# Retention scores and state products as 64-row matmuls of two heads into two PSUM banks

## The chip, the cores and the metric

The kernel runs on one core of a Trainium2 chip. The metric is device time in microseconds (us) for one execution. The engines are named as the profile names them: PE is TensorE (matmuls; PEld is its weight load), DVE is VectorE, ACT is ScalarE, POOL is GpSimd, and SP is the queue that issues all DMAs of this kernel.

## The reference

One layer of a streaming encoder over 2048 prompt tokens and 64 sample tokens, model width 1024. Three groups of heads (HGRN2, retention, memory cross-attention) take their columns from one projection of the normalised input; each is multiplied by a gate, and the concatenation goes through an output projection and a final norm. The part at issue is retention: 4 heads, keys of 64, values of 128, in chunks with a carried state.

```
scores = einsum('bcihd,bcjhd->bchij', qc, kc) * intra      # gamma^|n-m| inside a chunk
o  = einsum('bchij,bcjhv->bcihv', scores, vc)
dr = einsum('bcjhd,hj,bcjhv->bchdv', kc, k_decay, vc)
r_{c+1} = chunk_decay * r_c + dr_c                         # the state of each head, 64 x 128
o  = o + einsum('bcihd,hi,bchdv->bcihv', qc, q_decay, r_c)
o_rt = head_group_norm(o, g) * silu(gate)                  # mean and variance over the 128 of a head
```

All results are fp32. The kernel uses chunks of 128 tokens with a mask in the decay table that reproduces the reference's chunks of 64.

## The kernel before

The tokens are worked in two groups of 1024 and 1088 (the second ends with the 64 sample tokens), and within a group projection by projection: retention's gates, then its values, then its queries and keys, then HGRN2, then attention; the output projection comes last. Projections are long runs of matmuls in which a number is split into a high and a low part, three products for one (`gemm_col`, L249, and `gemm_tok`, L294). They make up most of TensorE's work. Everything else is hung between them.

The order on PE and SP is written out by hand. A planner holds a clock, `now`, that is advanced by `pe(us)` behind each matmul with the cost that the author gives it. Side work is a generator that is put up as a task with a due time; each `yield d` ends one section and makes the next due `d` later. `poll()` is called between the steps of a projection (in `gemm_tok` after every three passes of 512 columns but the last three) and runs what is due, earliest first; a section of a task waits until the task before it of the same class is past the same section. The order on DVE, ACT and POOL is chosen by the scheduler of the language, which prefers the sections of tasks.

`retention` (L586) computes the projection of one chunk of 128 tokens, applies the rotary embedding (L602 to L608), makes the decayed keys `kd` (L610), and puts up `retention_tail` (L615), due 6.0 us later. The tail has four sections:

- Section 0: four transposes (L620) put q and k of four heads into a bank `tr` as pairs: rows 0 to 63 hold an even head, rows 64 to 127 the odd one. ACT copies q into `q2` as a block-diagonal (L624, L625): even head in columns 0 to 127 of the upper rows, odd head in columns 128 to 255 of the lower rows, and zeros elsewhere. ACT copies k (L628), DVE makes q times its decay (L630).
- Section 1: for each pair `p` one 128-row matmul of 256 columns gives the scores of two heads at once (L637; four small ones for the sample, L635). All four heads fill the one bank `scb`. DVE multiplies by the decay table into `sd` (L641). Four matmuls on 64 columns of the array each (L647) give the state's increment `db`, two heads in the upper and two in the lower partitions.
- Section 2: for each pair one 128-row matmul with the block-diagonal state `R` (L653), then the two heads' products of `sd` with the values accumulate onto it (L657). All four heads fill the bank `ob`. DVE updates the state from `db` (L666, four operations; L662 in the first chunk, which has no state and no L653), reduces `ob` (L673), scales (L674) and subtracts the mean (L677); ACT squares (L682), POOL takes the power (L237), DVE multiplies (L685).
- Section 3: four transposes (L693), the product with the gate (L695), and a store.

PSUM has eight banks of 512 fp32 columns. `acc()` hands out three, `trp()` two (tag `tr`), `obank()` two (tag `ob`, used for `db` and `ob`, and by HGRN2 and attention), and `scb` is one bank of its own that HGRN2 uses as well. A new tile from a pool waits until a bank of it has been read for the last time.

Of the kernel before, what the change touches and what calls it, by code (L numbers as in the profile page):

```python
# [11 lines left out]
ALU = mybir.AluOpType  # L12
AX = mybir.AxisListType
PSUM = bass.MemoryType.PSUM

P = 128
# [37 lines left out]
D_RT0 = 6.0  # L54
# [9 lines left out]
def layer_kernel(ctx: ExitStack, tc: tile.TileContext, io: dict):  # L64
    nc = tc.nc
    V, S, G, T = nc.vector, nc.scalar, nc.gpsimd, nc.tensor
# [25 lines left out]
    def pe(us):  # L92
        now[0] += us

    def task(cls, gen, delay):
        prev = last.get(cls)
        t = {"t": now[0] + delay, "gen": gen, "prev": prev, "stage": 0}
        last[cls] = t
        pend.append(t)
# [107 lines left out]
    for i in range(2):  # L207
        a = const.tile([P, 512], F32, name=f"abuf{i}")
# [4 lines left out]
    scb = p_sc.tile([P, 512], F32, name="scb")  # L213
# [6 lines left out]
    def slot(dt=F32):  # L220
        return wk.tile([P, 512], dt, tag="s", name="s")
# [7 lines left out]
    def trp():  # L229
        return p_tr.tile([P, 512], F32, tag="tr", name="tr")  # L230

    def obank():
        return p_o.tile([P, 512], F32, tag="ob", name="ob")
# [176 lines left out]
    def subchunks(tok0, nt):  # L410
        out = []
        o = 0
        while o < nt:
            L = 128 if tok0 + o < SEQ else DEC
            out.append((o, L))
            o += L
        return out
# [8 lines left out]
    def bc(ap, shape):  # L426
        return ap.to_broadcast(shape)
# [158 lines left out]
    def retention(ws, ht, tok0, nt, vt, R, dtab, last_tile):  # L586
        for c, (o, L) in enumerate(subchunks(tok0, nt)):
            t = tok0 + o
            ti = t // 128
            ct_ = sm.tile([P, 96], F32, tag="cs", name="cs", bufs=2)  # L590
            dma(ct_[0:L], io["rope"][ti, 0:L])
            cosb = ct_[0:L, 0:32].rearrange("p (a b) -> p a b", a=1)
            nsin = ct_[0:L, 32:64].rearrange("p (a b) -> p a b", a=1)
            sinb = ct_[0:L, 64:96].rearrange("p (a b) -> p a b", a=1)
            ps = gemm_tok(ws, ht, o, L, last_tile and o + L == nt)
            if L == DEC:
                pf = slot()
                fold(pf[0:L], ps)
                ps = pf
            r = slot()  # L600
            tmp = slot()
            V.tensor_tensor(out=r[0:L].rearrange("p (a b) -> p a b", b=32), in0=ps[0:L].rearrange("p (a b) -> p a b", b=32),  # L602
                            in1=bc(cosb, [L, 16, 32]), op=ALU.mult)
            pv = ps[0:L].rearrange("p (a t b) -> p a t b", t=2, b=32)
            tv = tmp[0:L].rearrange("p (a t b) -> p a t b", t=2, b=32)
            V.tensor_tensor(out=tv[:, :, 0, :], in0=pv[:, :, 1, :], in1=bc(nsin, [L, 8, 32]), op=ALU.mult)
            V.tensor_tensor(out=tv[:, :, 1, :], in0=pv[:, :, 0, :], in1=bc(sinb, [L, 8, 32]), op=ALU.mult)
            V.tensor_tensor(out=r[0:L], in0=r[0:L], in1=tmp[0:L], op=ALU.add)  # L608
            kd = slot()
            V.tensor_tensor(out=kd[0:L, 0:256].rearrange("p (h d) -> p h d", h=4), in0=r[0:L, 256:512].rearrange("p (h d) -> p h d", h=4),  # L610
                            in1=bc(kdec[L][0:L].rearrange("p (h o) -> p h o", o=1), [L, 4, 64]), op=ALU.mult)
            task("rt", retention_tail(t, L, vt[c], r, kd, R[0 if L == 128 else 1], dtab), D_RT0)
            poll()

    def retention_tail(t, L, v, r, kd, R, dtab):  # L615
        first = t == 0
        sample = L == DEC
        tr = trp()
        for j in range(4):
            T.transpose(tr[:, j * 128:j * 128 + L], r[0:L, j * 128:(j + 1) * 128], ident[0:L, 0:L])  # L620
            pe(0.107)
        trv = tr.rearrange("p (j l) -> p j l", j=4)
        q2 = q2b[(t // 128) % 2]
        S.copy(q2[0:64, :, 0:L], trv[0:64, 0:2, 0:L])  # L624
        S.copy(q2[64:128, :, 128:128 + L], trv[64:128, 0:2, 0:L])  # L625
        kq = slot()
        kqv = kq.rearrange("p (a b) -> p a b", a=4)
        S.copy(kqv[:, 0:2, 0:L], trv[:, 2:4, 0:L])  # L628
        if not first:
            V.tensor_tensor(out=kqv[:, 2:4, 0:L], in0=trv[:, 0:2, 0:L], in1=qdec[:, :, 0:L], op=ALU.mult)  # L630
        yield D_RT1
        for p in range(2):
            if sample:
                for hh in range(2):
                    T.matmul(scb[0:L, p * 256 + hh * 128:p * 256 + hh * 128 + L], kqv[:, p, 0:L], q2[:, p, hh * 128:hh * 128 + L], start=True, stop=True)  # L635
            else:
                T.matmul(scb[:, p * 256:(p + 1) * 256], kqv[:, p, :], q2[:, p, :], start=True, stop=True)  # L637
            pe(0.426)
        sd = slot()
        sdv = sd.rearrange("p (a b) -> p a b", a=4)  # L640
        V.tensor_tensor(out=sdv[0:L, :, 0:L], in0=scb.rearrange("p (a b) -> p a b", a=4)[0:L, :, 0:L],  # L641
                        in1=dtab.rearrange("p (a b) -> p a b", a=4)[0:L, :, 0:L], op=ALU.mult)
        db = obank()
        dv = db[:, 0:256].rearrange("p (a b) -> p a b", a=2)
        for h in range(4):
            p, hh = h // 2, h % 2
            T.matmul(dv[64 * hh:64 * hh + 64, p, :], kd[0:L, h * 64:(h + 1) * 64], v[0:L, h * 128:(h + 1) * 128], start=True, stop=True)  # L647
            pe(0.213)
        yield D_RT2
        ob = obank()  # L650
        for p in range(2):
            if not first:
                T.matmul(ob[0:L, p * 256:(p + 1) * 256], kqv[:, 2 + p, 0:L], R[:, p, :], start=True, stop=False)  # L653
                pe(0.426)
            for hh in range(2):
                h = 2 * p + hh
                T.matmul(ob[0:L, h * 128:(h + 1) * 128], sdv[0:L, h, 0:L], v[0:L, h * 128:(h + 1) * 128], start=first, stop=first or hh == 1)  # L657
                pe(0.213)
        for hh in range(2):
            sl = slice(64 * hh, 64 * hh + 64)  # L660
            if first:
                V.tensor_copy(R[sl, :, 128 * hh:128 * hh + 128], dv[sl])  # L662
            else:
                for p in range(2):
                    blk = R[sl, p, 128 * hh:128 * hh + 128]
                    V.scalar_tensor_tensor(out=blk, in0=blk, scalar=gcol[L][sl, p:p + 1], in1=dv[sl, p, :], op0=ALU.mult, op1=ALU.add)  # L666
        if sample or t + 128 == SEQ:
            dst = io["o_srt_s"] if sample else io["o_srt_p"]
            for h in range(4):
                p, hh = h // 2, h % 2  # L670
                store(dst[0, 0, h], R[64 * hh:64 * hh + 64, p, 128 * hh:128 * hh + 128], 2.0)
        mu = small(4, "mu")
        V.tensor_reduce(out=mu[0:L], in_=ob[0:L].rearrange("p (a b) -> p a b", a=4), axis=AX.X, op=ALU.add)  # L673
        V.tensor_scalar(out=mu[0:L], in0=mu[0:L], scalar1=1.0 / 128, scalar2=None, op0=ALU.mult)  # L674
        cc = slot()
        ccv = cc[0:L].rearrange("p (a b) -> p a b", a=4)
        V.tensor_tensor(out=ccv, in0=ob[0:L].rearrange("p (a b) -> p a b", a=4),  # L677
                        in1=bc(mu[0:L].rearrange("p (a o) -> p a o", o=1), [L, 4, 128]), op=ALU.subtract)
        ss = small(4, "ss4")
        junk = slot()  # L680
        for h in range(4):
            S.activation(junk[0:L, h * 128:(h + 1) * 128], cc[0:L, h * 128:(h + 1) * 128], AF.Square, accum_out=ss[0:L, h:h + 1])  # L682
        rs = small(4, "rs4")
        rsqrt_small(rs[0:L], ss[0:L], 4, 1.0 / 128, EPS)
        V.tensor_tensor(out=ccv, in0=ccv, in1=bc(rs[0:L].rearrange("p (a o) -> p a o", o=1), [L, 4, 128]), op=ALU.mult)  # L685
        gr = slot()
        grv = gr.rearrange("p (a b) -> p a b", a=4)[:, :, 0:L]
        blk = mixT[1024:1536, t:t + L].rearrange("(a p) l -> p a l", p=P)
        dma(grv, blk)
        yield D_RT3  # L690
        tro = trp()
        for h in range(4):
            T.transpose(tro[:, h * 128:h * 128 + L], cc[0:L, h * 128:(h + 1) * 128], ident[0:L, 0:L])  # L693
            pe(0.107)
        V.tensor_tensor(out=grv, in0=grv, in1=tro.rearrange("p (a b) -> p a b", a=4)[:, :, 0:L], op=ALU.mult)  # L695
        store(blk, grv)
# [153 lines left out]
    start = ExitStack()  # L850
# [341 lines left out]
    for i_, o in enumerate(order):  # L1192
        L = 128 if o < SEQ else DEC
# [113 lines left out]
```

## Time and profile before

| | us |
|---|---|
| median of 3 runs | 1943.49 |
| lowest and highest run | 1939.63, 1945.09 |
| the profiled execution | 1944.17 |
| its span, first to last instruction | 1942.4 |
| PE busy | 1908.9 |
| DVE busy | 1043.3 |
| ACT busy | 585.9 |

The granted TensorE clock was 0.995 over the span. In a row of a timeline stand the start in us, the duration, engine, line, operation, the tiles out<-in, the form of the array that is used (rows*columns), the operands' shape and a count; neighbours of one line are merged. A duration of a PE record holds the latency of the pipeline and overlaps with the next, so what a matmul costs is read from start to start. An fp32 matmul stands as two records. Rows of groups show busy time, mean ns of one, and the engine's idle time ahead of them with what ended it. Rows of one source line show durations in ns as lowest/median/highest, then the first and last start.

### The profile page before, as it was taken

The page shows a single profiled execution, that of the slowest core. Times are in us where ns is not written, and L with a number is a line of the kernel's source. Part 1 is how long each engine was busy: PE and PEld are TensorE (multiplying, and loading weights), DVE is VectorE, ACT ScalarE, POOL GpSimd, SP SyncE. Part 2 cuts the span into 40 slices and gives each one's busy share as a digit, 9 for nine tenths or more (in the row PEclk, how much of TensorE's full clock was granted, in tenths as well). Part 3 has the DMA queues.
Part 4 walks back from the last instruction along what each step waited for, and adds up shares of the span by engine and source line. Part 5 has one row for each costly group of instructions (what it writes and reads, how often), then busy time and mean ns, then how long its engine had stood idle before and what let it go on. Part 6 is the DMA issues. An engine that isn't in the chain of part 4 may idle for free.

```text
span 1942.4 us, 28116 instructions
## 1 busy us (share of the span) xinstructions
PE 1908.9 (98%) x10938; PEld 1618.5 (83%) x10938; DVE 1043.3 (54%) x2512; ACT 585.9 (30%) x1414; POOL 139.9 (7%) x335
## 2 busy tenths in 40 slices
PE   8999999999999999999999999999999999999998
PEld 7888788888888787988789998899989878888886
DVE  8527457753677557417637774477765642222222
ACT  7413232322333434312323332233333431111111
POOL 0001000000100100000101111021100000000000
PEclk9999999999999999999999999999999999999999
DMA  7512222111111424212211111111122342233322
GB/s 254 179 58 55 75 66 61 44 50 44 44 55 55 153 71 134 92 55 58 87 47 49 49 49 49 44 49 49 60 71 78 118 144 87 87 102 113 89 71 60
DMA packets 116742, 153.21 MB, mean 79 GB/s; under 512 B 13312, under 2 KB 79232, under 8 KB 116608
## 3 DMA queue, kind: packets, MB, share of 16 engines
q1 hardware_dynamic: 116608, 151.41, 25.4%
q8 instruction: 86, 1.41, 0.3%
q14 instruction: 48, 0.39, 0.1%
HBM read 117.69 MB, written 33.69 MB: 78 GB/s over the span
## 4 chain that ended last, share of the span: by engine, by line
PE 87%; DVE 6%; DMA 2%; ACT 2%; issue 1%; POOL 1%; SPq 0%; DVEq 0%; POOLq 0%; ACTq 0%
PE acc L249 39%; PE acc L1180 19%; PE acc L294 15%; PE scb L522 2%; PE ob L531 2%; PE ob L563 1%; PE ob L566 1%; PE acc L785 1%; PE ob L741 1%; PE acc L264 1%; PE tr L516 1%; PE tr L581 1%; PE tr L763 1%; DVE wlo L241 1%; ACT s L682 1%
## 5 line engine op out<-in xcount | busy, mean ns | idle before, releaser
L249 PE MATMUL acc<-hb,whi 128*128 128x320 f32 (+2 forms) x1696 | 409.1, 331 | 0.4 <-DVE hb L371 0.4
L249 PE MATMUL acc<-ha,whi 128*128 128x512 f32 x1120 | 354.7, 398 | 0.0
L249 PEld LDWEIGHTS acc<-hb,whi 128*128 128x128 f32 x1696 | 284.6, 189 | 25.0 <-issue 4.4
L241 DVE TENSOR_TENSOR wlo<-wst,whi 128x1024 fp32r<-128x1024 f32 x115 | 140.0, 1226 | 261.2 <-ACT whi L240 260.2
L249 PE MATMUL acc<-hb,wlo 128*128 128x256 f32 (+2 forms) x848 | 276.9, 327 | 0.0
L249 PEld LDWEIGHTS acc<-ha,whi 128*128 128x128 f32 x1120 | 205.0, 189 | 41.3 <-issue 2.6
L249 PE MATMUL acc<-ha,wlo 128*128 128x512 f32 x560 | 220.0, 393 | 0.0
L240 ACT CAST whi<-wst 128x1024 fp32r<-128x1024 f32 x115 | 119.7, 1051 | 211.4 <-PE acc L249 172.0
L249 PEld LDWEIGHTS acc<-hb,wlo 128*128 128x128 f32 x848 | 160.2, 189 | 11.2
L294 PE MATMUL acc<-whi,ha 128*128 128x512 f32 x512 | 161.0, 396 | 0.0
L294 PE MATMUL acc<-whi,hb 128*128 128x512 f32 x512 | 160.0, 394 | 0.0
L1180 PE MATMUL acc<-whi,s 128*128 128x512 f32 x396 | 125.9, 396 | 1.3 <-ACT s L240 1.0
L249 PEld LDWEIGHTS acc<-ha,wlo 128*128 128x128 f32 x560 | 105.7, 189 | 23.1 <-DVE wlo L241 0.2
L294 PEld LDWEIGHTS acc<-whi,hb 128*128 128x128 f32 x512 | 94.5, 188 | 19.8 <-issue 1.2
L294 PEld LDWEIGHTS acc<-whi,ha 128*128 128x128 f32 x512 | 93.8, 188 | 19.6 <-issue 1.3
L294 PE MATMUL acc<-wlo,ha 128*128 128x512 f32 x256 | 100.1, 391 | 0.0
L294 PE MATMUL acc<-wlo,hb 128*128 128x512 f32 x256 | 99.8, 390 | 0.0
L1180 PE MATMUL acc<-hb,s 128*128 128x512 f32 x400 | 97.7, 400 | 0.0
L1180 PE MATMUL acc<-ha,s 128*128 128x512 f32 x400 | 96.3, 396 | 0.0
L1180 PEld LDWEIGHTS acc<-hb,s 128*128 128x128 f32 x400 | 76.3, 191 | 18.4
L241 DVE TENSOR_TENSOR s<-mst,s 128x512 fp32r<-128x512 f32 (+1 forms) x64 | 40.4, 671 | 94.2 <-ACT s L240 94.2
L1180 PEld LDWEIGHTS acc<-whi,s 128*128 128x128 f32 x396 | 74.3, 188 | 19.6 <-ACT s L240 1.3
(236 smaller groups left out, 2913.3 us busy)
## 6 DMA issues: line engine op xcount, KB each, us to landing
wst<-w_in_t SPq DMA_DIRECT2D x104, 512.0 KB, 4.0
mixT<-s SPq DMA_DIRECT2D x64, 256.0 KB, 4.3
mst<-mixT SPq DMA_DIRECT2D x30, 512.0 KB, 5.9
wst<-w_out_t SPq DMA_DIRECT2D x16, 512.0 KB, 4.0
xq<-x_prompt SPq DMA_DIRECT2D x18, 256.0 KB, 5.0
o_yp<-xq SPq DMA_DIRECT2D x18, 256.0 KB, 2.3
s<-mixT SPq DMA_DIRECT2D x16, 256.0 KB, 3.0
s<-x_prompt SPq DMA_DIRECT2D x16, 256.0 KB, 5.3
```

Of the source, the lines that this page charges most:

```text
L240: S.copy(hi, src)
L241: V.tensor_tensor(out=lo, in0=src, in1=hi.bitcast(F32), op=ALU.subtract)
L249: T.matmul(ps[:, 0:nt], w[a][:, kk, :], ht[b][:, kk, 0:nt], start=(n == 0), stop=(n == 23))
L264: T.matmul(ps[:, 0:nt], w[a][:, kk, :], ht[b][:, kk, 0:nt], start=(kk == 0 and a + b == 0), stop=(kk == KT - 1 and a == 1))
L294: T.matmul(ps[0:L, :], ht[b][:, kk, o:o + L], w[a][:, kk % 2, :], start=(n == 0), stop=(n == 23))
L516: T.transpose(trk[:, c * 128:(c + 1) * 128], kch[:, c * 128:(c + 1) * 128], ident)
L522: T.matmul(scb[32 * e:32 * e + 32, c * 128 + 32 * e:(c + 1) * 128], K[:, c * 128 + 32 * e:c * 128 + 32 * e + 32], Qe[:, c, E_OFF[e]:E_OFF[ ...
L531: T.matmul(db[:, c * 128:(c + 1) * 128], kT[:, c * 128:(c + 1) * 128], vt[c], start=True, stop=True)
L563: T.matmul(ob[:, c * 128:(c + 1) * 128], A[:, c * 128:(c + 1) * 128], vt[c], start=True, stop=first)
L566: T.matmul(ob[:, c * 128:(c + 1) * 128], qst[:, c * 128:(c + 1) * 128], st[c][0], start=False, stop=True)
L581: T.transpose(tro[:, c * 128:(c + 1) * 128], on[:, c * 128:(c + 1) * 128], ident)
L1180: T.matmul(ps, m[a][:, kk % 4], w[b], start=(n == 0), stop=(n == 16 * len(terms) - 1))
```

## The change

The scores and the state products are no longer taken for two heads at once through zeros, but one matmul per head on 64 rows of the array (`sl`, rows 0 to 63 for the even head of a pair, 64 to 127 for the odd one), with 128 columns where there were 256. The even heads' results go into one bank and the odd heads' into another: `scb` and a bank of `obank()` for the scores, a bank of `obank()` and one of `trp()` for the outputs. For the sample the state product stays at 128 rows. `q2` holds the pair as it comes, so one ACT copy replaces two. Three DVE operations (L641, L673, L677) become two each. The planner's cost for a pair goes from 0.426 to 0.3, and the sample's tail is put up 2.0 us later.

```
-            task("rt", retention_tail(...), D_RT0)
+            task("rt", retention_tail(...), D_RT0 if L == 128 else D_RT0 + 2.0)
...
-        S.copy(q2[0:64, :, 0:L], trv[0:64, 0:2, 0:L])
-        S.copy(q2[64:128, :, 128:128 + L], trv[64:128, 0:2, 0:L])
+        S.copy(q2[:, :, 0:L], trv[:, 0:2, 0:L])
...
+        sc2 = (scb, obank())
         for p in range(2):
-            if sample:
-                for hh in range(2):
-                    T.matmul(scb[0:L, p * 256 + hh * 128:p * 256 + hh * 128 + L], kqv[:, p, 0:L], q2[:, p, hh * 128:hh * 128 + L], start=True, stop=True)
-            else:
-                T.matmul(scb[:, p * 256:(p + 1) * 256], kqv[:, p, :], q2[:, p, :], start=True, stop=True)
-            pe(0.426)
+            for hh in range(2):
+                sl = slice(64 * hh, 64 * hh + 64)
+                T.matmul(sc2[hh][0:L, p * 128:p * 128 + L], kqv[sl, p, 0:L], q2[sl, p, 0:L], start=True, stop=True)
+            pe(0.3)
...
-        V.tensor_tensor(out=sdv[0:L, :, 0:L], in0=scb.rearrange("p (a b) -> p a b", a=4)[0:L, :, 0:L],
-                        in1=dtab.rearrange("p (a b) -> p a b", a=4)[0:L, :, 0:L], op=ALU.mult)
+        for hh in range(2):
+            V.tensor_tensor(out=sdv[0:L, hh:4:2, 0:L], in0=sc2[hh].rearrange("p (a b) -> p a b", a=4)[0:L, 0:2, 0:L],
+                            in1=dtab.rearrange("p (a b) -> p a b", a=4)[0:L, hh:4:2, 0:L], op=ALU.mult)
...
-        ob = obank()
+        ob2 = (obank(), trp())
         for p in range(2):
             if not first:
-                T.matmul(ob[0:L, p * 256:(p + 1) * 256], kqv[:, 2 + p, 0:L], R[:, p, :], start=True, stop=False)
-                pe(0.426)
+                for hh in range(2):
+                    sl = slice(0, P) if sample else slice(64 * hh, 64 * hh + 64)
+                    T.matmul(ob2[hh][0:L, p * 128:(p + 1) * 128], kqv[sl, 2 + p, 0:L], R[sl, p, 128 * hh:128 * hh + 128], start=True, stop=False)
+                pe(0.3)
             for hh in range(2):
                 h = 2 * p + hh
-                T.matmul(ob[0:L, h * 128:(h + 1) * 128], sdv[0:L, h, 0:L], v[0:L, h * 128:(h + 1) * 128], start=first, stop=first or hh == 1)
+                T.matmul(ob2[hh][0:L, p * 128:(p + 1) * 128], sdv[0:L, h, 0:L], v[0:L, h * 128:(h + 1) * 128], start=first, stop=True)
...
-        V.tensor_reduce(out=mu[0:L], in_=ob[0:L].rearrange("p (a b) -> p a b", a=4), axis=AX.X, op=ALU.add)
+        for hh in range(2):
+            V.tensor_reduce(out=mu[0:L, hh:4:2], in_=ob2[hh][0:L, 0:256].rearrange("p (a b) -> p a b", a=2), axis=AX.X, op=ALU.add)
...
-        V.tensor_tensor(out=ccv, in0=ob[0:L].rearrange("p (a b) -> p a b", a=4),
-                        in1=bc(mu[0:L].rearrange("p (a o) -> p a o", o=1), [L, 4, 128]), op=ALU.subtract)
+        for hh in range(2):
+            V.tensor_tensor(out=ccv[:, hh:4:2, :], in0=ob2[hh][0:L, 0:256].rearrange("p (a b) -> p a b", a=2),
+                            in1=bc(mu[0:L, hh:4:2].rearrange("p (a o) -> p a o", o=1), [L, 2, 128]), op=ALU.subtract)
```

More of the change, by code (lines that the diff above doesn't have):

```diff
@@ L611, in retention @@
                             in1=bc(kdec[L][0:L].rearrange("p (h o) -> p h o", o=1), [L, 4, 64]), op=ALU.mult)
-            task("rt", retention_tail(t, L, vt[c], r, kd, R[0 if L == 128 else 1], dtab), D_RT0)
+            task("rt", retention_tail(t, L, vt[c], r, kd, R[0 if L == 128 else 1], dtab), D_RT0 if L == 128 else D_RT0 + 2.0)
             poll()
```

## The prediction

> **What bounds the kernel now.** I read the page first, its busy table and its chain of waits.
>
> ```profile
> span 1942.4 us, 28116 instructions
> ...
> PE 1908.9 (98%) x10938; PEld 1618.5 (83%) x10938; DVE 1043.3 (54%) x2512; ACT 585.9 (30%) x1414; POOL 139.9 (7%) x335
> ...
> PE 87%; DVE 6%; DMA 2%; ACT 2%; issue 1%; POOL 1%; SPq 0%; DVEq 0%; POOLq 0%; ACTq 0%
> ```
>
> TensorE is busy nearly throughout and carries the chain. So two things count: how long TensorE takes for the edited matmuls, and every moment in which it has to stand still, since all later passes queue behind. Next, the stretches in which retention runs, one per group of tokens (columns: stretch, its length, then busy time and count for PE, PEld, DVE, ACT, POOL).
>
> ```profile
> 130.00:228.00 98.00, 94.25 (x515) 76.72 (x515) 63.95 (x130) 24.43 (x95) 9.90 (x17) 1.00 0.27 80
> 860.00:975.00 115.00, 110.12 (x591) 87.69 (x590) 72.89 (x152) 28.07 (x108) 12.16 (x20) 0.99 0.29 84
> ```
>
> Here too TensorE is the bound. It is idle 98.00 - 94.25 = 3.8 us and 115.00 - 110.12 = 4.9 us, 8.6 us in all, and VectorE has about a third of its time free. Then the two edited matmuls in the groups by line:
>
> ```profile
> L653 PE MATMUL ob<-r,s 128*128 128x256 f32 x60 | 17.9, 380 | 0.0
> L637 PE MATMUL scb<-q2b,s 128*128 128x256 f32 x64 | 17.7, 401 | 2.9 <-ACT s L628 2.8
> ```
>
> 64 records are 16 prompt chunks x 2 matmuls x 2 passes (an fp32 matmul shows as two), and 60 are 15 chunks (the first has no state). Durations of single records hold the pipeline's latency, so I price by starts, in the timeline of PE around one chunk.
>
> ```profile
> 142.33 0.40 PE L294 MATMUL acc<-wlo,ha 128*128 128x512 f32 x1
> 142.56 1.03 PE L637 MATMUL scb<-q2b,s 128*128 128x256 f32 x4
> 143.52 0.66 PE L647 MATMUL ob<-v,s 128*64 128x128 f32 x8
> 144.11 0.73 PE L294 MATMUL acc<-whi,ha 128*128 128x512 f32 x2
> 144.68 0.40 PE L294 MATMUL acc<-wlo,ha 128*128 128x512 f32 x1
> 144.92 0.60 PE L620 MATMUL tr<-cst,s 128*128 128x128 f32 x4
> ```
>
> ```profile
> 888.25 0.60 PE L653 MATMUL ob<-r,s 128*128 128x256 f32 x2
> 888.69 0.61 PE L657 MATMUL ob<-v,s 128*128 128x128 f32 x4
> ...
> 889.56 0.61 PE L657 MATMUL ob<-v,s 128*128 128x128 f32 x4
> 890.01 1.03 PE L637 MATMUL scb<-q2b,s 128*128 128x256 f32 x4
> 891.02 0.66 PE L647 MATMUL ob<-v,s 128*64 128x128 f32 x8
> ```
>
> The unit prices. A state product (L653, two passes) takes 888.69 - 888.25 = 0.44 us, so 0.22 a pass of 256 columns; L657 takes 890.01 - 889.56 = 0.45 for four, so 0.11 a pass of 128. L637 has four passes of 0.22 but takes 143.52 - 142.56 = 0.96: 0.08 more, and what follows it is L647, which uses half the array's columns (form 128*64). I read the rest as the price of emptying the array before its shape changes. L647 itself has eight passes of 0.11, which in a row are 0.88, yet it takes 144.11 - 143.52 = 0.59: the passes of its two column halves run side by side, four slots of 0.11, and 0.15 remains for its first, uncovered weight load (64 columns, 0.05) and for emptying again (0.10). I take 0.09 for one emptying. The L294 passes behind start 144.68 - 144.11 = 0.57 apart for two where 0.23 each (142.33 to 142.56) makes 0.46: the first 128-column weight load after a change of shape is uncovered and costs 0.11.
>
> Does a half in rows cost the same as a half in columns? The trace has one row form at work, the sample's transposes at L693:
>
> ```profile
> 969.40 0.39 PE L294 MATMUL acc<-wlo,ha 128*128 128x512 f32 x1
> 969.72 0.46 PE L693 MATMUL tr<-cst,s 64*128 64x64 f32 x4
> 970.11 0.74 PE L294 MATMUL acc<-whi,ha 128*128 128x512 f32 x2
> 970.69 0.40 PE L294 MATMUL acc<-wlo,ha 128*128 128x512 f32 x1
> ```
>
> 969.72 - 969.40 = 0.32 where 0.23 is usual: 0.09 on the way in. Behind it, 970.69 - 970.11 = 0.58: 0.12 for the uncovered load. So yes, both ways. What no row shows is two row halves side by side. I take it from the nearest row, L647's column halves (paired); the other bound is passes in a row, as in L657.
>
> **The change part by part.** The profiled execution took 1944.17 us, 1.8 around its span; the median of the runs is 1943.49. I sum against 1944.17 and take 0.7 off.
>
> *Scores.* Before: 0.96. After: empty 0.09, load 0.11, four slots of 0.11, empty 0.09 (L647 still needs another shape) = 0.73. Saved 0.23 x 16 = 3.7 us; the sample's one small block is left out. If the halves don't pair: 0.09 + 0.11 + 0.88 + 0.09 = 1.17, a loss of 0.21 x 16 = 3.4.
>
> *State products.* Each of the two per chunk now stands alone between 128-row matmuls. Before 0.44. After: empty 0.09, load 0.11, two slots 0.22, empty 0.09, and an uncovered load for L657, 0.11 = 0.62. Lost 0.18 x 30 = 5.4 us. Unpaired: 0.84, lost 0.40 x 30 = 12.0. So the matmuls alone come to +1.7 us, unpaired to +15.4.
>
> The Trainium skill ("TensorEngine Tiling", Theoretical Speedup) gives up to 2x for a contraction of 64 rows or fewer. By it alone the scores would take 0.48 and a state product 0.22, 14 us less in all; it prices neither emptying nor loads there. The trace agrees for column halves (0.59 for L647 against 0.88); for row halves no run here shows it yet.
>
> *PSUM.* The pool behind obank() has two banks. Before, a chunk took two, db and ob, so each new db waited for the previous chunk's db to be read (L666) and each ob for the previous ob. Now it takes three: second score bank, db, ob. The order stays scores, db, ob chunk by chunk, so the next chunk's second score bank has to wait for the last db (L666), and its db for the last ob, whose last reader is the subtraction at L677. That comes late on VectorE. Its timeline over the same chunk as above:
>
> ```profile
> 890.00 0.97 DVE L666 SCALAR_TENSOR_TENSOR r<-r,cst,ob 64x128 f32<-64x128 f32 x3
> 891.00 0.69 DVE L673 TENSOR_REDUCE mu<-ob 128x4 f32<-128x512 f32 x1
> 891.72 0.42 DVE L607 TENSOR_TENSOR s<-acc,cs 128x256 f32<-128x256 f32 x1
> 892.06 0.16 DVE L674 TENSOR_SCALAR mu<-mu 128x4 f32<-128x4 f32 x1
> 892.18 0.69 DVE L608 TENSOR_TENSOR s<-s 128x512 f32<-128x512 f32 x1
> 892.79 0.68 DVE L695 TENSOR_TENSOR s<-s,tr 128x512 f32<-128x512 f32 x1
> 893.38 0.42 DVE L610 TENSOR_TENSOR s<-s,cst 128x256 f32<-128x256 f32 x1
> 893.72 0.68 DVE L677 TENSOR_TENSOR s<-ob,mu 128x512 f32<-128x512 f32 x1
> 894.32 0.68 DVE L641 TENSOR_TENSOR s<-scb,s 128x512 f32<-128x512 f32 x1
> ```
>
> TensorE is ready for db at 890.01 + 0.73 = 890.74. The ob bank comes free when the first half of the subtraction is done: 893.72, plus 0.15 for the divided reduction ahead of it, plus 0.42 = 894.29. A stall of 3.6 us, with the db matmuls and every projection pass queued behind it. The shortest case is the first chunk of all:
>
> ```profile
> 149.02 1.03 PE L637 MATMUL scb<-q2b,s 128*128 128x256 f32 x4
> 150.15 0.69 DVE L677 TENSOR_TENSOR s<-ob,mu 128x512 f32<-128x512 f32 x1
> ```
>
> ```profile
> L677 DVE TENSOR_TENSOR s<-ob,mu x17: 680/691/693, 150.1 to 965.2; 128x512 f32<-128x512 f32 x16, 64x512 f32<-64x512 f32 x1
> ```
>
> 150.15 + 0.57 - (149.02 + 0.73) = 1.0. Of the 17 subtractions, 11 are followed by the next scores within 1.5 us. I step the planner's clock through with the new costs (each pair of edited matmuls 0.6 in place of 0.852): the order stays, but after the third chunk of each group the scores come one slot of three passes (0.69) later. With that, the same reckoning for the eleven gives 1.0, 2.9, 1.6, 2.6, 3.5 in the first group and 1.5, 3.6, 1.6, 2.6, 2.1, 1.7 in the second: 24.7 us. In the other six, four passes of L294 or more lie between and hide it. I take 20, because the VectorE queue ahead of L677 will be a little shorter once TensorE stands still; bounds 0, if the scheduler's order or its choice of bank happens to avoid it, and 25. The Trainium skill ("TensorEngine Tiling", Restrictions and Gotchas) names this risk without a price: row tiling increases PSUM pressure, as its tiles write different banks. No run here shows yet whether that holds for this kernel.
>
> The ob half in the transposes' pool (trp, two banks) is held until the other half of L677, but the next transposes that reuse its bank lie at least two sections later: nothing, and a wait like db's, 1 us or more a time, if that cover fails.
>
> *VectorE and ScalarE.*
>
> ```profile
> L641 DVE TENSOR_TENSOR s<-scb,s x17: 407/681/692, 143.6 to 957.2; 128x512 f32<-128x512 f32 x16, 64x256 f32<-64x256 f32 x1
> L630 DVE TENSOR_TENSOR s<-tr,cst x16: 290/417/425, 146.9 to 951.3; 128x256 f32<-128x256 f32 x15, 128x128 f32<-128x128 f32 x1
> L624 ACT COPY q2b<-tr x17: 259/366/368, 140.0 to 950.5; 64x256 f32<-64x256 f32 x16, 64x128 f32<-64x128 f32 x1
> ```
>
> Each of three operations (L641, L673, L677) becomes two of half size: 2 x 417 - 681 = 0.15 us more, 0.45 a chunk, 7.7 us in all, in VectorE's free third; what of it delays L677 is in the stalls. ScalarE loses one copy of 0.37 a chunk, which shortens the way to the scores; TensorE waits for that way only in the 2.8 us beside L637 above. With both and VectorE catching up during the stalls, I put 2.5 of the present 8.6 us idle as given back (0 to 5).
>
> Sum: +1.7 + 20 - 2.5 = +19.2; 1944.17 + 19.2 - 0.7 = 1963.
>
> **The rivals.** *The bank waits vanish.* For it: banks are handed out by a scheduler, and VectorE's order may change. Against: three uses in two banks must reuse one early. Time: 1943.5 + 1.7 - 1 (little is given back then) = 1944.
>
> *Faster: the shapes change for free and the halves pair.* The mechanism is the one the edit aims at: no emptying, no uncovered loads, banks hidden. Scores 0.96 to 0.44 + 0.09 (as now, ahead of L647) = 0.53, 0.43 x 16 = 6.9; state products 0.44 to 0.22, 0.22 x 30 = 6.6; 13.5 in all, 1930. For it: L647's halves pair. Against: the 0.09 and 0.12 around the 64*128 form. It decides when the way in and out costs the 46 blocks less than 13.5 / 46 = 0.29 us each, where I reckon 0.20 for the scores and 0.40 for the products, and the stalls less than what is left. The Trainium skill's 2x ("TensorEngine Tiling", Theoretical Speedup) stands on this side.
>
> *The row halves don't pair*, because their weight loads, as long as a pass (0.11), follow one another. Against: L647's loads pair. Time: 1943.5 + 15.4 + 20 - 2.5 = 1976.
>
> **How the numbers follow.** Forecast (stalls, paired) 0.55, own range 1952 to 1972; waits vanish 0.20; faster 0.13; unpaired 0.12. Predicted 1963. The range leaves out the faster rival and the top of the unpaired one: 1941 to 1976. About 0.3% (5.8 us) is what a measurement of this kernel can tell from no change. Faster 0.13; same 0.18, the rival without waits but for its edge; slower 0.69.
>
> **What would show it.** Right: L647 waiting for L677 in eleven places, PE idle in the two stretches near 25 us against 8.6, scores 0.64 us from their first start to L647 with 0.09 more ahead of them, a state product still some 0.42 from its start to L657, but with 0.09 more ahead and 0.11 behind. Starts of the two heads' passes a few ns apart show pairing; 0.11 apart refute it. The forecast is wrong if L647 waits only for L666, or if no time is lost where a 64*128 block meets a 128*128 one.

## The result and the profile after

The changed kernel takes 1963.09 us (median of 6 runs, 1956.68 to 1964.09), the kernel before in the same comparison 1941.96. The ratio is 1.0097, with a 95% interval of 1.0076 to 1.0119: about 1% slower, at the forecast's number. The profiled execution took 1964.0 us. First its page, then its two retention stretches, with the columns as before:

```profile
span 1962.2 us, 28406 instructions
...
PE 1918.5 (98%) x11066; PEld 1621.4 (83%) x11066; DVE 1049.2 (53%) x2563; ACT 578.7 (29%) x1397; POOL 138.4 (7%) x335
```

```profile
130.00:245.00 115.00, 106.49 (x607) 83.92 (x606) 65.57 (x154) 21.53 (x88) 9.71 (x17) 0.96 0.24 67
870.00:997.00 127.00, 114.41 (x642) 87.90 (x641) 73.81 (x176) 23.50 (x99) 11.48 (x20) 0.93 0.23 66
```

The page alone hides the loss: PE is still at 98%. The stretches show it. TensorE is idle 8.5 + 12.6 = 21.1 us there, against 8.6 in the two stretches of before, and the third number from the right, the granted clock, has gone from 1.00 and 0.99 to 0.96 and 0.93. The forecast had not looked at that second change.

The first chunk's scores, in the timeline of PE (the lines have moved: scores are L635, db L646, state products L654, the values' products L658, the state update L667, the reduction L675, the subtraction L680):

```profile
141.25 0.39 PE L294 MATMUL acc<-wlo,ha 128*128 128x512 f32 x1
141.57 0.37 PE L635 MATMUL scb<-q2b,s 64*128 64x128 f32 x1
141.57 0.37 PE L635 MATMUL ob<-q2b,s 64*128 64x128 f32 x1
141.78 0.27 PE L635 MATMUL scb<-q2b,s 64*128 64x128 f32 x1
141.79 0.27 PE L635 MATMUL ob<-q2b,s 64*128 64x128 f32 x1
...
142.21 0.66 PE L646 MATMUL ob<-v,s 128*64 128x128 f32 x8
142.80 0.72 PE L294 MATMUL acc<-whi,ha 128*128 128x512 f32 x2
```

The two heads start together, so the row halves pair. From the first scores to db, 141.57 to 142.21, is 0.64 us, and 141.57 - 141.25 = 0.32 shows 0.09 more than a pass on the way in: 0.73 in place of 0.96. A state product:

```profile
153.94 0.37 PE L654 MATMUL ob<-r,s 64*128 64x128 f32 x1
153.94 0.37 PE L654 MATMUL tr<-r,s 64*128 64x128 f32 x1
...
154.36 0.49 PE L658 MATMUL ob<-v,s 128*128 128x128 f32 x2
...
155.00 0.37 PE L654 MATMUL ob<-r,s 64*128 64x128 f32 x1
```

Product and values together take 155.00 - 153.94 = 1.06 us, where 0.44 + 0.44 = 0.88 stood before. The product's own 0.42 hardly changed; the 0.64 of L658 holds the way back.

Now who made PE wait, in the changed kernel and then in the kernel before (total us, times, longest):

```profile
PE ob L646 <- DVE s L680: 16.4, 11, 2.7
...
PE tr L620 <- DVE s L608: 2.0, 1, 2.0
...
PE ob L635 <- DVE r L667: 1.2, 2, 1.0
...
PE scb L635 <- ACT s L627: 1.0, 1, 1.0
```

```profile
PE tr L620 <- DVE s L608: 2.9, 2, 1.8
PE scb L637 <- ACT s L628: 2.8, 1, 2.8
...
PE tr L693 <- DVE s L685: 1.4, 2, 0.8
...
PE tr L620 <- DVE s L630: 0.8, 1, 0.8
...
PE ob L647 <- DVE r L666: 0.6, 1, 0.6
```

db waits for the subtraction in eleven places, none of which was there before. One of them, the same chunk as in the forecast, on PE and on DVE:

```profile
900.02 0.49 PE L635 MATMUL scb<-q2b,s 64*128 64x128 f32 x2
900.51 0.37 PE L635 MATMUL ob<-q2b,s 64*128 64x128 f32 x1
...
903.37 1.12 PE L646 MATMUL ob<-v,s 128*64 128x128 f32 x8 [2.15 <-DVE s L680]
...
909.33 0.60 PE L620 MATMUL tr<-cst,s 128*128 128x128 f32 x4
```

```profile
899.48 0.98 DVE L667 SCALAR_TENSOR_TENSOR r<-r,cst,ob 64x128 f32<-64x128 f32 x3 [0.21 <-PE tr L654]
900.49 0.42 DVE L675 TENSOR_REDUCE mu<-ob 128x2 f32<-128x256 f32 x1
...
901.27 0.42 DVE L607 TENSOR_TENSOR s<-acc,cs 128x256 f32<-128x256 f32 x1
...
901.73 0.69 DVE L608 TENSOR_TENSOR s<-s 128x512 f32<-128x512 f32 x1
902.46 0.42 DVE L610 TENSOR_TENSOR s<-s,cst 128x256 f32<-128x256 f32 x1
902.80 0.42 DVE L680 TENSOR_TENSOR s<-ob,mu 128x256 f32<-128x256 f32 x1
```

L680's half on ob ends at 903.22 and L646 starts at 903.37. Ahead of it stand the next chunk's rotary embedding (L607, L608) and decayed keys (L610), though the transposes that need the former (L620) come only at 909.33. The second score bank waits too: L667 reads the last db until 899.48 + 0.98 = 900.46, and the odd head starts at 900.51, 0.49 us behind the even one, so that the first two passes run alone here.

What happens to the clock shows at the longest stall, on PE and then in the stretch over its end and in one over the end of a stall of 2.34 us:

```profile
159.96 1.12 PE L646 MATMUL ob<-v,s 128*64 128x128 f32 x8 [2.69 <-DVE s L680]
...
162.03 0.63 PE L294 MATMUL acc<-wlo,hb 128*128 128x512 f32 x1
162.46 1.05 PE L294 MATMUL acc<-whi,hb 128*128 128x512 f32 x2
```

```profile
159.00:165.80 6.80, 5.84 (x19) 4.56 (x20) 2.46 (x7) 1.28 (x8) 1.20 (x2) 0.50 0.21 53
196.60:200.00 3.40, 3.40 (x14) 2.59 (x15) 1.56 (x5) 2.20 (x9) 1.20 (x2) 0.51 0.04 7
```

A pass of 512 columns takes 162.46 - 162.03 = 0.43 us, nearly twice its 0.23. The granted clock is 0.50 for 6.8 us here and 0.51 for 3.4 us from 196.6 on. Over both retention stretches the clock that is missing comes to 0.04 x 115 + 0.07 x 127 = 13.5 us, that is some 27 us at half, in seven stretches. One of them, 3.4 us from 879.2 on, follows no wait for a bank but 1.98 us in which L620 waited for L608, a wait that the kernel before has as well. Over the whole span less is new: (1 - 0.991) x 1962.2 = 17.7 us are missing where (1 - 0.995) x 1942.4 = 9.7 were missing before, 8 us more. The six runs differ by it as well: the two short ones (1956.68 and 1958.36 us) had a mean clock of 0.994 and 0.995, the other four (1962.35 to 1964.09) 0.990 to 0.992.

The Trainium skill ("TensorE: Matmul & The Clock Gate", Part 1: The HAM clock gate) has TensorE fall to half its clock after an idle window of about 3.4 us and rise after a busy one; the rule that it draws is no idle gap over about 3.4 us. The halving (0.50) and the lengths (3.4 and 6.8 us) agree; the rule isn't enough here, where the half clock came with stalls of 2.7 and 2.34 us.

### The profile page after: what moved, and what is told of

Read it like the earlier page. It is cut to its first block, busy times and chain, and to the rows that moved or that the text cites. A ratio compares the mean times of both kernels' runs of the same rounds, so it can differ in the third digit from the quotient of the medians.

```text
span 1962.2 us, 28406 instructions
## 1 busy us (share of the span) xinstructions
PE 1918.5 (98%) x11066; PEld 1621.4 (83%) x11066; DVE 1049.2 (53%) x2563; ACT 578.7 (29%) x1397; POOL 138.4 (7%) x335
## 4 chain that ended last, share of the span: by engine, by line
PE 90%; DVE 5%; DMA 2%; ACT 1%; issue 1%; SPq 0%; POOL 0%; DVEq 0%; POOLq 0%; ACTq 0%
PE acc L249 39%; PE acc L1183 18%; PE acc L294 17%; PE scb L522 2%; PE ob L531 1%; PE ob L563 1%; PE ob L566 1%; PE acc L788 1%; PE ob L744 1%; PE acc L264 1%; PE tr L766 1%; PE tr L516 1%; PE tr L581 1%; PE ob L654 1%; DVE wlo L241 1%
## 5 line engine op out<-in xcount | busy, mean ns | idle before, releaser
L294 PE MATMUL acc<-whi,hb 128*128 128x512 f32 x512 | 165.1, 405 | 0.0
```

Of the source, the lines that this page charges most:

```text
L294: T.matmul(ps[0:L, :], ht[b][:, kk, o:o + L], w[a][:, kk % 2, :], start=(n == 0), stop=(n == 23))
```

## The experiments

The theory: the third use of two banks makes db wait for the subtraction, the waits also bring the halved clock, and the row halves' own price is small, a gain at the scores and a loss at the products. The main rival: the changes of the array's shape are the loss. The first four ran on one chip (kernel before there: 1943.48 us), the second four on one chip (1943.02 us). Every ratio is to the kernel before, with its 95% interval.

**own_banks.** The changed kernel with db's matmuls first and the odd scores in db's bank (the sample's in a bank of trp()).

```
+        db = obank()                      # and its four matmuls, ahead of the scores
-        sc2 = (scb, obank())
+        sc2 = (scb[:, 0:256], trp()[:, 0:256] if sample else db[:, 256:512])
```

> The changed kernel, with the odd heads' scores in columns 256 to 511 of the db bank and the db matmuls ahead of the scores, so that a chunk takes two banks of obank() as before the change; the row halves and every price of the matmuls stay. Theory (bank waits, and the halved clock behind them, are the loss): L646 no longer waits for L680, PE idle in retention falls back to 8 to 9 us, and the time comes to some 2 us over the kernel before, near 1944. Rival (the changes of the array's shape are the loss): the time stays near 1960.

Measured: 1942.98 us, ratio 1.0000 (0.9992 to 1.0009). Its retention stretches and its one wait for a bank of obank():

```profile
130.00:235.00 105.00, 102.29 (x601) 80.67 (x600) 65.81 (x154) 21.89 (x89) 10.16 (x17) 0.98 0.27 79
860.00:980.00 120.00, 114.78 (x679) 89.41 (x678) 77.42 (x180) 26.20 (x102) 12.46 (x20) 0.99 0.29 82
```

```profile
PE ob L635 <- DVE r L667: 1.7, 4, 0.5
```

Idle is 2.7 + 5.2 = 7.9 us again (L635 is db here). With every row half, every change of shape and every divided VectorE operation still in place, the loss is gone. The main rival falls.

**banks_only.** The kernel before with a third use of obank() and nothing else of the matmuls touched.

```
+        sc2 = (scb, obank())              # p = 0 and p = 1, still 128 rows, 256 columns each
-                T.matmul(scb[:, p * 256:(p + 1) * 256], kqv[:, p, :], q2[:, p, :], start=True, stop=True)
+                T.matmul(sc2[p][:, 0:256], kqv[:, p, :], q2[:, p, :], start=True, stop=True)
```

> The kernel before, its matmuls of 128 rows unchanged, but the second pair's scores go into a bank of obank(), and the multiplication by the decay table is in two halves. The sample's tail is put up 2.0 us later, as in the change. Theory: L647 waits for the subtraction in about eleven places as in the changed kernel, 15 us of stalls less 4 given back and 4 of halved clock: 12 to 17 us over the kernel before, near 1956, with no matmul changed. Rival (shape changes): equal to the kernel before.

Measured: 1963.80 us, ratio 1.0102 (1.0088 to 1.0116).

```profile
PE ob L649 <- DVE s L679: 19.3, 11, 2.8
...
PE ob L638 <- DVE r L668: 2.0, 3, 1.6
```

Eleven waits again, and the same loss as the change itself, without a single 64-row matmul. The expectation was some 8 us too low, and the waits are 21.3 us where it had 15. The planner's costs are the old ones here, so the slot that the change wins after the third chunk is missing; that this made the waits longer is not shown. The halved clock hardly appears in the profiled execution, though the longest wait is 2.8 us:

```profile
130.00:245.00 115.00, 103.59 (x549) 84.09 (x548) 64.95 (x138) 25.38 (x97) 9.71 (x17) 0.99 0.24 70
870.00:997.00 127.00, 112.63 (x600) 89.46 (x599) 72.96 (x159) 27.77 (x108) 11.48 (x20) 0.99 0.24 68
```

So the waits alone can make a loss of this size, and equal stalls don't always bring the same clock.

**products_only.** Only the state products in 64-row form.

```
-                T.matmul(ob[0:L, p * 256:(p + 1) * 256], kqv[:, 2 + p, 0:L], R[:, p, :], start=True, stop=False)
+                    T.matmul(ob2[hh][0:L, p * 128:(p + 1) * 128], kqv[sl, 2 + p, 0:L], R[sl, p, 128 * hh:128 * hh + 128], start=True, stop=False)
```

> The kernel before with only the state products in 64-row form, outputs in a bank of obank() and one of trp(), reduction and subtraction in halves; scores as before, no third use of obank(). Theory: 30 products lose 0.18 us each, 5.4 us in all, near 1947, and no wait of L647 for the subtraction. Rival (changes of shape are free): 6 us gained, near 1936. Second rival (banks of trp() are held too long): over 1950, with transposes waiting for the subtraction.

Measured: 1947.62 us, ratio 1.0019 (1.0010 to 1.0028), a loss of 2 to 5.4 us. Its list of PE waits names the subtraction nowhere. Transposes wait 3.1 us for a bank of trp() that L630 still reads, where it was 0.8, but the tail's waits together stay where they were, 8.3 us against 8.5. So this half of the change loses by itself, as worked out, with the estimate of 5.4 at the interval's upper end; half a matmul's rows saved don't pay for two changes of shape around 0.22 us of work.

**scores_only.** own_banks with the products as before the change.

```
-        ob2 = (obank(), trp())            # 64-row products
+        ob = obank()                      # 128-row products, reduction and subtraction whole
```

> As own_banks, with the state products back as 128-row matmuls of two heads into one bank, and reduction and subtraction whole again. Theory: scores alone gain 0.23 us x 16 = 3.7 us, so 3 to 5 us under the kernel before, near 1938, a ratio of 0.998. Rival (row halves cost as much as they save): equal to the kernel before within 0.1%.

Measured: 1939.62 us, ratio 0.9983 (0.9973 to 0.9993): 1.4 to 5.2 us gained, and below both kernels. The scores' gain of 3.7 us lies in the middle of that, though the net holds other things too: one ScalarE copy less, and a wait of db for the state update, which is longer than before (0.6) because db now comes a scores' length earlier:

```profile
PE ob L635 <- DVE r L665: 6.1, 9, 2.4
```

**scores_tr.** The attempt to take that wait away.

```
-        sc2 = (scb[:, 0:256], trp()[:, 0:256] if sample else db[:, 256:512])   # db ahead of it
+        sc2 = (scb, trp())                # scores ahead of db again
```

> Scores in 64-row form, scores ahead of db as in the change, the odd heads' in a bank of trp(); state products of 128 rows and one ob bank as before. So obank() has two uses a chunk again and db does not come earlier than before. scores_only still showed 6.1 us of db matmuls waiting for the state update. Theory: those waits go, of which about half shows in the time: 1936 to 1938. Rival (banks of trp() are then short): transposes wait, 1941 or more.

Measured: 1940.75 us, ratio 0.9992 (0.9982 to 1.0001). A miss: not to be told from the kernel before, nor clearly from scores_only. The wait shrank to 1.6 us in three places, but others came:

```profile
PE tr L692 <- DVE s L629: 3.7, 1, 3.7
PE scb L635 <- ACT s L627: 3.2, 1, 3.2
```

A transpose waits for a bank of trp() once, as the rival had it, and the scores once for ScalarE. What lies behind the second was not followed up.

**interleaved.** own_banks in an order with twice the changes of shape.

```
-        # db p0, db p1, scores p0, scores p1
+        # db p0, scores p0, db p1, scores p1
```

> As own_banks, the same matmuls in another order: first pair's db matmuls, first pair's scores, second pair's db, second pair's scores. That adds, per chunk, one way into 64-column form and one into 64-row form, 0.09 + 0.05 and 0.09 + 0.11, and no work. Theory: 0.34 us x 16 = 5.4 us over own_banks, near 1948. Rival (changes of shape cost nothing): equal to own_banks, 1943.

Measured: 1946.80 us, ratio 1.0029 (1.0018 to 1.0040), against own_banks at 1.0000: by the ratios 5.6 us more for the same work. One chunk of it, by the starts of its four blocks:

```profile
142.36 0.44 PE L637 MATMUL ob<-v,s 128*64 128x128 f32 x4
142.73 0.37 PE L641 MATMUL scb<-q2b,s 64*128 64x128 f32 x1
...
143.15 0.44 PE L637 MATMUL ob<-v,s 128*64 128x128 f32 x4
143.52 0.37 PE L641 MATMUL scb<-q2b,s 64*128 64x128 f32 x1
...
143.94 0.73 PE L294 MATMUL acc<-whi,ha 128*128 128x512 f32 x2
```

143.94 - 142.36 = 1.58 us, where the two blocks in one piece are 0.59 (L646) and 0.64 (L635): 0.35 more, as reckoned from the way in (0.09 each) and the loads, and 0.35 x 16 = 5.6 us. This is the price of two changes of shape by themselves.

**unpaired.** own_banks with both heads on rows 0 to 63; the odd heads' scores are computed from the even heads' data.

```
-                T.matmul(sc2[hh][0:L, p * 128:p * 128 + L], kqv[sl, p, 0:L], q2[sl, p, 0:L], start=True, stop=True)
+                T.matmul(sc2[hh][0:L, p * 128:p * 128 + L], kqv[0:64, p, 0:L], q2[0:64, p, 0:L], start=True, stop=True)
```

> As own_banks, but the odd heads' scores read rows 0 to 63 as the even heads' do, so the odd heads' scores are computed from the even heads' data and two heads can't run side by side. Theory (halves pair): the scores take eight slots of 0.11 where they took four, 0.43 us x 16 = 6.9 us over own_banks, near 1950. Rival (the halves' weight loads follow one another anyway): equal to own_banks.

Measured: 1949.86 us, ratio 1.0042 (1.0030 to 1.0054), by the ratios 8 us over own_banks.

```profile
142.25 0.48 PE L640 MATMUL scb<-q2b,s 64*128 64x128 f32 x2
142.57 0.38 PE L640 MATMUL ob<-q2b,s 64*128 64x128 f32 x2
...
143.33 0.72 PE L294 MATMUL acc<-whi,ha 128*128 128x512 f32 x2
```

The scores take 143.33 - 142.25 = 1.08 us in place of 0.64, 0.44 more, or 7 us in 16 chunks. Pairing is what makes the row halves worth anything, and it needs different rows.

**filled.** The changed kernel with useless work in the stalls.

```
+        for _ in range({1: 1, 2: 5, 3: 1, 5: 4, 6: 1, 9: 1, 10: 4, 11: 1, 13: 4, 14: 3, 16: 2}.get(t // 128, 0)):
+            # the four score matmuls once more, into the same places
```

> The changed kernel with work added: in the eleven chunks in which L646 waits, the scores are computed again, one to five times over (27 times in all, 0.43 us each), between the scores and the db matmuls, so that TensorE has passes to do for most of the 16.4 us of waiting. Theory (the stalls cost their own length and, where they last 2 us or more, a halved clock afterwards): the stalls' length stays, the halved clock in the retention stretches goes from 27 us to 10 or less, and the time falls by 4 to 9 us in spite of the added work, to 1954 to 1959. Rival (the clock has no part in it): 1963 or more.

Measured: 1955.14 us, ratio 1.0069 (1.0057 to 1.0081). That is 8 us under the change by the medians and 5 by the ratios (1.0097 less 1.0069; the two intervals overlap a little), with 27 x 0.43 = 11.6 us of passes more.

```profile
PE ob L651 <- DVE s L685: 4.3, 10, 0.6
```

```profile
130.00:245.00 115.00, 111.75 (x715) 89.62 (x714) 66.37 (x154) 22.12 (x89) 9.71 (x17) 0.99 0.25 70
870.00:997.00 127.00, 120.35 (x795) 94.62 (x794) 73.56 (x176) 24.55 (x100) 11.48 (x20) 1.00 0.22 64
```

Waiting (4.3 us) and added work together are as long as the waits they replace (16.4), and the granted clock is back at 0.99 and 1.00. So in the changed kernel TensorE's standing still cost some 5 to 8 us beyond its own length; the granted clock shows why, but the size is not sharp.

## Why the prediction was right, point by point

- *Scores*, 0.73 and 3.7 us gained: 0.73 in the trace; scores_only shows 1.4 to 5.2 us, with other waits in it.
- *State products*, 0.18 lost each, 5.4 us: 1.06 - 0.88 = 0.18 in the trace; products_only shows 2 to 5.4 us. That the halves pair was taken from L647's column halves, and held; unpaired shows what it is worth.
- *PSUM*, L646 waiting for the subtraction in eleven places, 20 us: eleven places, 16.4 us, and 1.2 us of the odd scores for L667, which the forecast named and did not price. The stalls came shorter than the list of 24.7. The reason given there, a shorter VectorE queue, fits the chunk shown: from the state update to the subtraction VectorE took 902.80 - 899.48 = 3.32 us, where 893.72 - 890.00 = 3.72 stood before; for the other ten it is not shown. No transpose waited for the half in trp(), as said. own_banks and banks_only show that these waits are the loss, from both sides.
- *The planner's order*, one slot more after the third chunk of each group: so it came.
- *Given back*, 2.5 of 8.6 us: the waits of the tail's other matmuls went from 8.5 us (the five rows of before) to 3.6 (2.0 and 1.0 in the rows above, and 0.6 of transposes waiting for L629), so 4.9 came back.
- *The sum* had +1.7 + 20 - 2.5 = 19.2. By the traces it is +1.7 + 17.6 - 4.9 = 14.4, and then the halved clock, 5 to 8 us by filled and at most some 8 by the clock that is missing. The medians differ by 21.1, and by the ratio it is 18.8. So the number was met with one term missing, the halved clock, and two terms that were off in the same direction by 2.4 us each made room for it. The mechanism was right; the exact agreement was luck. None of the three rivals came: the waits are there, the changes of shape cost time, and the halves pair.

## What to carry to other kernels

Count a pool's uses per round against its banks, and follow the reader that frees each bank down its own engine's queue: a third use of two banks cost 1% here, and moving the new tile into the unused half of a bank that is already held cost nothing. Before taking a matmul apart into halves of the array, add the price of the way in and out from the trace, and group what shares a shape: four passes on each half of the rows, next to another divided block, paid; two, alone between undivided matmuls, did not. When TensorE is the bound, a stall can cost more than its length: look at the granted clock of the stretch behind it.

## What the runs showed of the hardware

The halves' two heads start within 0.01 us of each other (141.57 and 141.57, 141.78 and 141.79), although each load of 128 columns, where nothing covers it, costs as much as a pass (0.11 us). A change of shape costs 0.09 us (141.57 - 141.25, less a pass of 0.23), read here as emptying, plus the first load of the new shape (0.11 for 128 columns); interleaved confirms the sum by time, 0.35 us for two. Around the end of a TensorE stall of 2.7 us a stretch of 6.8 us at half clock began, and around that of one of 2.34 us a stretch of 3.4. A stall of 1.54 us, ended at 950.2, had a half-clock stretch behind it from 950.9 on, while one of 2.53 us in banks_only, ended at 197.6, had none; which stalls bring the half clock isn't settled by these runs.
